# Last attention of a fused block stack: outputs with tokens on partitions, scaled per pair of heads and then transposed; gains folded into k and the rope tables

## The chip, the cores and the metric

The kernel runs on one core of one Trainium2 chip. The metric is the device time of one execution in microseconds, which is that of its only core. Five engines run side by side, each through its own list of instructions in order: TensorE (PE in the profile, its weight loads PEld), VectorE (DVE), ScalarE (ACT), GpSimd (POOL) and SyncE (SP), which issues the transfers from device memory.

## The reference

A stream of 256 tokens of width 1024 goes through two stacks of blocks. The change touches only the last attention, a sliding-window one with 16 query heads and 2 key/value heads of width 64, rope on the first 16 of the 64 columns, and one learned sink per head:

```
q = rms_norm_2(q, q_gain); k = rms_norm_2(k, k_gain)
q = apply_partial_rope(q, cos, sin); k = apply_partial_rope(k, cos, sin)
...
scores = jnp.einsum('bntkgd,bnskd->bnkgts', qb, k_band).astype(jnp.float32) * (HEAD_DIM ** -0.5)
mask = (k_pos >= 0) & (k_pos <= q_pos) & (q_pos - k_pos < WINDOW)      # WINDOW = BLOCK = 128
scores = jnp.where(mask[None, :, None, None], scores, -jnp.inf)
m = jnp.maximum(jnp.max(scores, axis=-1, keepdims=True), sink)
p = jnp.exp(scores - m)
probs = p / (jnp.sum(p, axis=-1, keepdims=True) + jnp.exp(sink - m))
o = jnp.einsum('bnkgts,bnskd->bntkgd', probs.astype(v_band.dtype), v_band)
return o.reshape(b, s, SW_Q_HEADS * HEAD_DIM) @ w_out
```

With 256 tokens there are two blocks of 128 queries. The first sees 128 keys, the second 256.

## The kernel before

All matrix products with weights are done in three matmuls, of a high and a low part of both sides (`mm3`, the lines L398 to L400). A weight tile `raw` comes by DMA, ACT writes its high part `wh` (L224), DVE the low part `wl` (L225). A product of activations needs the same split of the activations: `hilo` lets ACT write `ah` (L494) and DVE `al` (L495).

The stage in question is `window`. `in_fill` computes q, k and v (four groups of four query heads, and one group for k and v). `normed` makes the normed and rotated q or k of a group: DVE multiplies by the inverse norm (L1099), then the gain (L1101) and rope (L1104 to L1107) follow, on DVE for k and on POOL for the four groups of q. `transposed` turns the result over on PE (L1115) and lets ACT copy it (L1118).

Then come 16 heads in a software pipeline. Each head has four steps:

- s1: for an even head PE computes the scores `s` of it and of the next head (L1208, L1210), two heads at once since each uses 64 rows of the array. For every head DVE adds the mask and takes the row minimum of the negated scores (L622), ACT takes the exponentials `p` with their sums (L625), and the sink's term `es` (L1216).
- s1b: DVE adds the sink's term, takes the reciprocal and scales `p` by it (L1223 to L1226).
- s2: PE transposes `p` in three blocks (L1233), ACT copies them to `pt` (L1235).
- s3, for odd heads only: four matmuls with v as the stationary side and `pt` moving (L1245, L1247) give the outputs `o` of the pair, with the 64 columns of each head on partitions and the tokens along the rows; the two heads go to the two halves of the partitions. `hilo` splits them into `ah` and `al`, the pair's entry in `mix`.

No scheduler moves anything: the engines run in the order in which the code calls them. `pipeline` sets it. In round t it calls, by `SW_ORDER = "013..2"` and the lags (1, 2, 4): s1 of head t, s1b of head t-1, s3 of head t-4, then twice the filler, then s2 of head t-2. The filler is a generator of other matmuls, at first the rest of q, then `rows_steps`, the product of `mix` with the output weights: for pair c it takes two steps (tokens 0 to 127, then 128 to 255; six matmuls each) as soon as `mix[c]` is set in the program, which is when the instructions that make it have been written down, not when they have run. PE's matmuls wait for `ah` and `al` by semaphore. For the last four pairs the steps go another way: first the first half of the tokens of pairs 4 to 7, and at the end the second half.

Tiles in the eight PSUM banks come from two rings of four: `gbank` (ring "g") gives `s`, `pT`, `tp`, `o`; a new tile of a ring waits until the tile four requests earlier has been read.

## Time and profile before

| | us |
|---|---|
| three runs | 1604.93, 1600.98, 1604.84 (median 1604.84) |
| profiled execution, its own time | 1600.43 |
| its span (what the trace covers) | 1598.7 |
| PE busy in the span | 1582.0 (99%) |
| DVE, ACT, POOL busy | 967.4 (61%), 819.7 (51%), 46.9 (3%) |
| chain of work that ended last, by engine | PE 92%, DVE 5%, ACT 2% |

The stage `window` lies between about 1320 and 1405 us of the span. PE's busy time counts matmuls from start to a modelled end, so the work of a group is read better from the start of one group to the start of the next. In a row of the timeline, what stands in square brackets is how long the engine was idle before it and who released it; "x4" merges four records. One fp32 matmul of the program is two records on PE in these rows where its inputs are full fp32 (scores, outputs), and one for the split products.

### The profile page before, as it was taken

What the parts mean: (1) busy time and instruction counts of PE and PEld (TensorE: products, weight loads), DVE (VectorE), ACT (ScalarE), POOL (GpSimd) and SP (SyncE); (2) the same over time, 40 slices, a digit from 0 to 9 for tenths busy, and PEclk for the clock granted to TensorE, in tenths of its full rate; (3) what the DMA queues carried; (4) which work ended last, traced back from release to release, by engine and by line L of the source; (5) the groups of instructions that cost most, each with busy time, mean ns of one, the idle gap of its engine ahead of it and who ended that gap; (6) DMA issues with size and microseconds to landing.
All of it is one profiled execution on the core that took longest, in us unless ns stands there. A gap on an engine that the chain in (4) does not pass through costs nothing.

```text
span 1598.7 us, 27739 instructions
## 1 busy us (share of the span) xinstructions
PE 1582.0 (99%) x11230; PEld 1453.6 (91%) x11230; DVE 967.4 (61%) x1637; ACT 819.7 (51%) x1405; POOL 46.9 (3%) x70
## 2 busy tenths in 40 slices
PE   9999999999999999999999999999999999999999
PEld 8989999998799998999999889999999998699998
DVE  7786655578665556754564465555654558865553
ACT  6665444457554444544457765444444446754442
POOL 0101000000000000000000000000000002000000
PEclk9999999999999999999999999999999999999999
DMA  8545555553456554656545437556465554246552
GB/s 301 175 137 179 200 199 184 177 185 96 125 177 210 188 181 159 210 200 197 186 146 183 133 109 247 184 183 203 161 199 192 196 173 134 88 149 211 183 178 75
DMA packets 78946, 279.47 MB, mean 175 GB/s; under 512 B 9057, under 2 KB 10593, under 8 KB 78818
## 3 DMA queue, kind: packets, MB, share of 16 engines
q1 hardware_dynamic: 78050, 276.12, 52.6%
q0 software_dynamic: 768, 1.57, 0.5%
q8 instruction: 88, 1.44, 0.4%
q14 instruction: 40, 0.33, 0.1%
HBM read 276.61 MB, written 1.05 MB: 174 GB/s over the span
## 4 chain that ended last, share of the span: by engine, by line
PE 92%; DVE 5%; ACT 2%; issue 1%; DMA 1%; POOL 0%; SPq 0%; DVEq 0%; ACTq 0%; POOLq 0%
PE gu L398 16%; PE gu L400 16%; PE gu L399 16%; PE o L398 9%; PE o L399 9%; PE o L400 9%; DVE wl L225 2%; PE s L810 2%; PE k L398 1%; PE k L399 1%; PE k L400 1%; PE q L398 1%; PE q L399 1%; PE q L400 1%; PE v L398 1%; PE tp L368 1%
## 5 line engine op out<-in xcount | busy, mean ns | idle before, releaser
L225 DVE TENSOR_TENSOR wl<-raw,wh 128x1024 fp32r<-128x1024 f32 (+2 forms) x510 | 600.0, 1219 | 115.4 <-ACT wh L224 114.9
L398 PE MATMUL gu<-hh,wh 128*128 128x256 f32 x1920 | 540.4, 281 | 0.0
L400 PE MATMUL gu<-hl,wh 128*128 128x256 f32 x1920 | 539.6, 281 | 0.0
L399 PE MATMUL gu<-hh,wl 128*128 128x256 f32 x1920 | 539.1, 281 | 0.0
L224 ACT ACTIVATE wh<-raw 128x1024 fp32r<-128x1024 f32 (+2 forms) x510 | 506.5, 1043 | 44.8 <-DMA raw<-in_w_dram 26.6
L399 PEld LDWEIGHTS gu<-hh,wl 128*128 128x128 f32 x1920 | 361.9, 189 | 4.0
L398 PEld LDWEIGHTS gu<-hh,wh 128*128 128x128 f32 x1920 | 361.6, 188 | 4.0
L400 PEld LDWEIGHTS gu<-hl,wh 128*128 128x128 f32 x1920 | 361.8, 188 | 0.0
L552 ACT ACTIVATE sg<-gu 128x256 f32<-128x256 f32 x120 | 45.9, 383 | 426.3 <-PE gu L400 415.2
L398 PE MATMUL o<-wh,ah 128*128 128x512 f32 x656 | 260.0, 396 | 0.4 <-ACT ah L494 0.4
L399 PE MATMUL o<-wh,al 128*128 128x512 f32 x656 | 257.8, 393 | 0.0
L400 PE MATMUL o<-wl,ah 128*128 128x512 f32 x656 | 257.7, 393 | 0.0
L553 DVE TENSOR_TENSOR sg<-gu,sg 128x256 f32<-128x256 f32 x120 | 50.9, 424 | 295.9 <-ACT sg L552 295.8
L400 PEld LDWEIGHTS o<-wl,ah 128*128 128x128 f32 x656 | 123.1, 188 | 27.0
L398 PEld LDWEIGHTS o<-wh,ah 128*128 128x128 f32 x656 | 123.7, 189 | 25.6 <-issue 2.8
L399 PEld LDWEIGHTS o<-wh,al 128*128 128x128 f32 x656 | 123.2, 188 | 22.6 <-DVE al L495 0.5
L494 ACT ACTIVATE ah<-sg 128x256 fp32r<-128x256 f32 x120 | 50.1, 418 | 71.0 <-DVE sg L553 71.0
L495 DVE TENSOR_TENSOR al<-sg,ah 128x256 fp32r<-128x256 f32 x120 | 51.0, 425 | 58.1 <-ACT ah L494 58.1
L625 ACT ACTIVATE p<-p,mn 128x256 f32<-128x256 f32 x96 | 46.1, 481 | 30.3 <-DVE mn L622 30.1
L494 ACT ACTIVATE hh<-tp 128x512 fp32r<-128x512 f32 x40 | 23.2, 597 | 61.5 <-PE tp L368 61.3
L398 PE MATMUL gu<-wh,hh 128*128 128x256 f32 x192 | 54.7, 285 | 0.0
L399 PE MATMUL gu<-wh,hl 128*128 128x256 f32 x192 | 54.0, 282 | 0.0
(249 smaller groups left out, 1888.4 us busy)
## 6 DMA issues: line engine op xcount, KB each, us to landing
raw<-in_w_dram SPq DMA_DIRECT2D x498, 512.0 KB, 4.5
gb<-in_gains_dram SPq DMA_DIRECT2D x10, 512.0 KB, 5.0
raw<-in_w_dram SPq DMA_DIRECT2D x8, 416.0 KB, 5.3
hank<-in_t_dram SPq DMA_DIRECT2D x8, 192.0 KB, 4.2
hank<-in_rpb_dram POOLq DMA_DIRECT2D x16, 96.0 KB, 4.4
out_dram<-x SPq DMA_DIRECT2D x4, 256.0 KB, 2.0
raw<-in_w_dram SPq DMA_DIRECT2D x2, 384.0 KB, 4.7
x<-in_x_dram SPq DMA_DIRECT2D x2, 256.0 KB, 3.0
```

The costliest lines, as they stand in the source:

```text
L224: ACT.activation(out=hi, in_=src, func=AF.Copy)
L225: late.append(lambda: engine.tensor_tensor(out=lo, in0=src, in1=hi.bitcast(F32), op=ALU.subtract))
L368: PE.transpose(ps[:, k * 128:(k + 1) * 128], xn[:, k * 128:(k + 1) * 128], ident)
L398: PE.matmul(ps, lhsT=lh, rhs=rh, start=first, stop=False)
L399: PE.matmul(ps, lhsT=ll, rhs=rh, start=False, stop=False)
L400: PE.matmul(ps, lhsT=lh, rhs=rl, start=False, stop=last)
L494: ACT.activation(out=hi, in_=src, func=AF.Copy)
L495: DVE.tensor_tensor(out=lo, in0=src, in1=hi.bitcast(F32), op=ALU.subtract)
L552: ACT.activation(out=sg, in_=ps[:, 0:256], func=AF.Silu)
L553: DVE.tensor_tensor(out=sg, in0=ps[:, 256:512], in1=sg, op=ALU.mult)
L625: ACT.activation(out=p[:, sl], in_=p[:, sl], func=AF.Exp, scale=-1.0, bias=mn[:, b:b + 1], accum_out=sm[:, b:b + 1])
L810: PE.matmul(ps[:, i * 256:(i + 1) * 256], lhsT=q[pr, i * 128:(i + 1) * 128], rhs=k[pr, :], start=True, stop=True)
```

## The change

Three things change in `window` (and in `prepare_rope`, which fills tables much earlier, in the first feed-forward stage).

Outputs: `pt` becomes the stationary side and v the moving one. Per pair there are six matmuls of 64 columns in place of four (of 256 and 128 columns), and their output `o` has the tokens on partitions. DVE scales it into a tile `y` by the reciprocal sums of both heads. In the next even head's s3, a new function `turn` transposes `y` in two blocks on PE, and `hilo` reads those blocks instead of `o`. The pipeline gets a 17th, empty task so that the last pair's `turn` is called.

Sums: `p` is not scaled any more. The sink's term, its exponential, the sum and the reciprocal are computed once for a pair of heads (four columns) instead of once per head.

Rope and gains: on the 48 columns without rope the q gain is multiplied into the k gain; on the 16 with rope both gains go into two rope tables. The multiplication of q by its gain falls away, and q's rope runs on DVE instead of POOL.

```
+        for which, c in ((1, R_KG), (0, R_QG)):
+            DVE.tensor_tensor(out=rope[:, which], in0=rope[:, 0], in1=row[:, c:c + 16].unsqueeze(1).unsqueeze(1).to_broadcast([128, 2, 2, 16]),
+                              op=ALU.mult)
+        DVE.tensor_tensor(out=row[:, R_KG + 16:R_KG + 64], in0=row[:, R_KG + 16:R_KG + 64], in1=row[:, R_QG + 16:R_QG + 64], op=ALU.mult)
...
-        def normed(ps, heads, gcol, guess, engine=POOL):
+        def normed(ps, heads, which, guess):
...
-            engine.tensor_tensor(out=y3, in0=y3, in1=row[:, gcol:gcol + 64].unsqueeze(1).to_broadcast([128, n, 64]), op=ALU.mult)
+            if which:
+                DVE.tensor_tensor(out=y3[:, :, 16:64], in0=y3[:, :, 16:64],
+                                  in1=row[:, R_KG + 16:R_KG + 64].unsqueeze(1).to_broadcast([128, n, 48]), op=ALU.mult)
             t = wk.tile([128, 2, n, 16], F32, name="rts", tag="rtq", bufs=1)
             for j in range(2):
-                engine.tensor_tensor(out=t[:, j].rearrange("p (i h) d -> p i h d", i=2), in0=y[:, :, :, 0:16],
-                                     in1=rope[:, :, j].unsqueeze(2).to_broadcast([128, 2, heads, 16]), op=ALU.mult)
-            engine.tensor_tensor(out=y3[:, :, 0:8], in0=t[:, 0, :, 0:8], in1=t[:, 1, :, 8:16], op=ALU.subtract)
-            engine.tensor_tensor(out=y3[:, :, 8:16], in0=t[:, 0, :, 8:16], in1=t[:, 1, :, 0:8], op=ALU.add)
+                DVE.tensor_tensor(out=t[:, j].rearrange("p (i h) d -> p i h d", i=2), in0=y[:, :, :, 0:16],
+                                  in1=rope[:, which, :, j].unsqueeze(2).to_broadcast([128, 2, heads, 16]), op=ALU.mult)
+            DVE.tensor_tensor(out=y3[:, :, 0:8], in0=t[:, 0, :, 0:8], in1=t[:, 1, :, 8:16], op=ALU.subtract)
+            DVE.tensor_tensor(out=y3[:, :, 8:16], in0=t[:, 0, :, 8:16], in1=t[:, 1, :, 0:8], op=ALU.add)
...
-                mn, sm, rc, es = small(2, "mn"), small(2, "sm"), small(2, "rc"), small(2, "es")
-                softmax_rows(ps, WID, mn, p, sm, [cst[:, C_SW:C_SW + 256], cst[:, C_SW + 256:C_SW + 384]],
+                z = n % 2
+                if z == 0:
+                    state["sums"] = [small(4, name).rearrange("p (b z) -> p b z", z=2) for name in ("mn4", "sm4", "es4")]
+                mn, sm, es = state["sums"]
+                softmax_rows(ps, WID, mn[:, :, z], p, sm[:, :, z], [cst[:, C_SW:C_SW + 256], cst[:, C_SW + 256:C_SW + 384]],
                              start=nsink[:, n:n + 1])
-                ACT.activation(out=es, in_=mn, func=AF.Exp, bias=row[:, R_SI + n:R_SI + n + 1])
-                state[n] = p, sm, es, rc
+                state[n] = p
+                if z == 1:
+                    DVE.tensor_tensor(out=es, in0=mn, in1=row[:, R_SI + n - 1:R_SI + n + 1].unsqueeze(1).to_broadcast([128, 2, 2]),
+                                      op=ALU.add)
+                    ACT.activation(out=es, in_=es, func=AF.Exp)
+                    state["sums", n] = sm, es
...
             def s1b():
-                p, sm, es, rc = state[n]
-                DVE.tensor_tensor(out=sm, in0=sm, in1=es, op=ALU.add)
-                DVE.reciprocal(out=rc, in_=sm)
-                for b in range(2):
-                    DVE.tensor_scalar(out=p[:, WID[b]], in0=p[:, WID[b]], scalar1=rc[:, b:b + 1], scalar2=None, op0=ALU.mult)
-                state[n] = p
+                if n % 2:
+                    sm, es = state["sums", n]
+                    DVE.tensor_tensor(out=sm, in0=sm, in1=es, op=ALU.add)
+                    DVE.reciprocal(out=sm, in_=sm)
...
             def s3():
                 if h % 2 == 0:
+                    turn()
                     return
                 ps = gbank("o")
...
                 for z in range(2):
-                    PE.matmul(ps[PAIR[z], 0:256], lhsT=v[0], rhs=pts[z][:, 0:256], start=True, stop=False)
-                for z in range(2):
-                    PE.matmul(ps[PAIR[z], 128:256], lhsT=v[1], rhs=pts[z][:, 256:384], start=False, stop=True)
-                a = act_tiles()
-                hilo(ps[:, 0:256], *a)
-                mix[n // 2] = a
+                    o = ps[:, z * 64:z * 64 + 64]
+                    PE.matmul(o, lhsT=pts[z][:, 128:256], rhs=v[0], start=True, stop=False)
+                    PE.matmul(o, lhsT=pts[z][:, 256:384], rhs=v[1], start=False, stop=True)
+                    PE.matmul(ps[:, 128 + z * 64:192 + z * 64], lhsT=pts[z][:, 0:128], rhs=v[0], start=True, stop=True)
+                y = wk.tile([128, 2, 2, 64], F32, name="y", tag="v", bufs=3)
+                sm, _ = state.pop(("sums", n))
+                DVE.tensor_tensor(out=y, in0=ps[:, 0:256].rearrange("p (b z d) -> p b z d", b=2, z=2),
+                                  in1=sm.unsqueeze(3).to_broadcast([128, 2, 2, 64]), op=ALU.mult)
+                state["y"] = n // 2, y
...
+        def turn():
+
+            if "y" not in state:
+                return
+            k, y = state.pop("y")
+            ps = gbank("oT")
+            for b in range(2):
+                PE.transpose(ps[:, (1 - b) * 128:(2 - b) * 128], y[:, b].rearrange("p z d -> p (z d)"), ident)
+            a = act_tiles()
+            hilo(ps[:, 0:256], *a)
+            mix[k] = a
...
-        pipeline([head(n) for n in range(16)], fill, SW_RATE, SW_LAG, SW_ORDER)
+        pipeline([head(n) for n in range(16)] + [(nothing, nothing, nothing, turn)], fill, SW_RATE, SW_LAG, SW_ORDER)
```

Where this puts the instructions, at three places. First PE in round t = 10, where the scores of heads 10 and 11 are computed and the filler begins on the pair c = 2. The numbers after the names tell one tile from another. Before, from the outputs of that pair on:

```order
L1245 MATMUL o_15316<-pt_15220,v_14725 64x256
L1245 MATMUL o_15316<-pt_15260,v_14725 64x256
L1247 MATMUL o_15316<-pt_15220,v_14725 64x128
L1247 MATMUL o_15316<-pt_15260,v_14725 64x128
...
L1233 MATMUL pT_15336<-cst_64,p_15222 128x128 x3
L1208 MATMUL s_15342<-qk_14863,qk_15126 128x256
L1208 MATMUL s_15343<-qk_14863,qk_15126 128x256
L1210 MATMUL s_15342<-qk_14863,qk_15126 128x128
L1210 MATMUL s_15343<-qk_14863,qk_15126 128x128
L398 MATMUL o_15206<-wh_14905,ah_15321 128x512
L399 MATMUL o_15206<-wh_14905,al_15322 128x512
```

There ACT and DVE make `ah_15321` and `al_15322` straight from `o_15316`. Now, on PE in the same round:

```order
L1240 MATMUL pT_15296<-cst_64,p_15193 128x128 x3
L1210 MATMUL s_15302<-qk_14865,qk_15104 128x256
L1210 MATMUL s_15303<-qk_14865,qk_15104 128x256
L1212 MATMUL s_15302<-qk_14865,qk_15104 128x128
L1212 MATMUL s_15303<-qk_14865,qk_15104 128x128
L1272 MATMUL oT_15319<-cst_64,y_15283 128x128 x2
L398 MATMUL o_15177<-wh_14906,ah_15322 128x512
L399 MATMUL o_15177<-wh_14906,al_15323 128x512
```

The pair's first filler matmuls stood three groups (`pT`, `s` and a filler step) behind the outputs from which their input is made; now they stand right behind the two transposes from which it is made. So it is for the pairs 0 to 3.

Second, ACT in that round (`p` with its sums are the exponentials of a head, `pt` the copy of transposed probabilities, `wh` a weight split). Before:

```order
L625 ACTIVATE p_15302,sm_15304<-p_15302,mn_15303 128x256
L625 ACTIVATE p_15302,sm_15304<-p_15302,mn_15303 128x128
L1216 ACTIVATE es_15306<-mn_15303,row_65 128x2
L494 ACTIVATE ah_15321<-o_15316 128x256
L224 ACTIVATE wh_15333<-raw_14976 128x1024
L1235 ACTIVATE pt_15340<-pT_15336 128x384
L625 ACTIVATE p_15348,sm_15350<-p_15348,mn_15349 128x256
L625 ACTIVATE p_15348,sm_15350<-p_15348,mn_15349 128x128
```

Now, from the weight split of round 9 to the copy of round 10:

```order
L224 ACTIVATE wh_15293<-raw_14976 128x1024
L1242 ACTIVATE pt_15300<-pT_15296 128x384
L625 ACTIVATE p_15308,sm4_15310<-p_15308,mn4_15309 128x256
L625 ACTIVATE p_15308,sm4_15310<-p_15308,mn4_15309 128x128
L494 ACTIVATE ah_15322<-oT_15319 128x256
L1242 ACTIVATE pt_15336<-pT_15332 128x384
```

The split `ah` stood behind the exponentials of an odd head (9), whose scores had been computed a round earlier; now it stands behind those of the even head (10), whose scores are computed in this round.

Third, DVE in round 6, where the norm and rope of the last group of q fall. Before, between the split of pair 0 and the row minima of head 6:

```order
L495 TENSOR_TENSOR al<-o,ah 128x256
L290 TENSOR_TENSOR rt<-ry 128x8
L291 TENSOR_TENSOR rt<-rt,rh 128x8
L292 SCALAR_TENSOR_TENSOR rz<-rt,ry 128x8
L1099 TENSOR_TENSOR qn<-qkv,rz 128x256 x2
L622 ISA p,mn<-s,cst,nsink 128x256
```

Now, at the same place:

```order
L1259 TENSOR_TENSOR y<-o,sm_14990 128x256
L290 TENSOR_TENSOR rt<-ry 128x8
L291 TENSOR_TENSOR rt<-rt,rh 128x8
L292 SCALAR_TENSOR_TENSOR rz<-rt,ry 128x8
L1099 TENSOR_TENSOR qn<-qkv,rz 128x256 x2
L1106 TENSOR_TENSOR rts<-qn,rope 128x128 x2
L1108 TENSOR_TENSOR qn<-rts 128x8x8
L1109 TENSOR_TENSOR qn<-rts 128x8x8
L622 ISA p,mn_15161<-s,cst,nsink 128x256
```

The rope's four instructions have come in ahead of head 6's row minima, and the pair's `al` has gone behind them.

## Rows read from the trace of the kernel before

**Rows 1.** Windows of 2.5 us of the stage: us from the span's start, length, then busy time and instructions of PE, PEld, DVE, ACT and POOL, the granted TensorE clock, DMA share and GB/s.

```profile
1347.50:1350.00 2.50, 0.35 (x4) 0.22 (x4) 1.82 (x6) 1.17 (x4) 2.34 (x5) 1.00 0.59 152
...
1360.00:1362.50 2.50, 2.50 (x14) 1.42 (x12) 2.40 (x11) 2.09 (x8) 0.00 (x0) 0.53 0.65 177
...
1375.00:1377.50 2.50, 2.50 (x18) 1.85 (x17) 1.07 (x4) 2.35 (x8) 0.00 (x0) 1.00 0.67 210
```

**Rows 2.** Waits of PE between 1340 and 1400 us: engine, tile and line that waited, what it waited for, us in total, times, longest.

```profile
PE s L1208 <- ACT qk L1118: 2.1, 1, 2.1
PE pT L1233 <- DVE p L1226: 1.7, 2, 1.1
PE tp L1115 <- DVE al L495: 0.8, 1, 0.8
PE o L1245 <- ACT pt L1235: 0.7, 2, 0.4
PE s L1208 <- DVE mn L622: 0.6, 1, 0.6
PE s L1208 <- ACT pt L1235: 0.4, 1, 0.4
PE o L398 <- ACT ah L494: 0.4, 1, 0.4
```

**Rows 3.** Timeline of PE in the steady part, one pair: start, us, engine, line, operation, tiles, shape, count.

```profile
1376.21 0.49 PE L1233 MATMUL pT<-cst,p 128*128 128x128 f32 x3
1376.63 0.70 PE L1208 MATMUL s<-qk 64*128 64x256 f32 x4
...
1377.48 0.50 PE L398 MATMUL o<-wh,ah 128*128 128x512 f32 x1
...
1378.98 0.49 PE L1233 MATMUL pT<-cst,p 128*128 128x128 f32 x3
1379.40 0.65 PE L1245 MATMUL o<-pt,v 128*64 128x256 f32 x4
...
1380.20 0.50 PE L398 MATMUL o<-wh,ah 128*128 128x512 f32 x1
```

**Rows 4.** Timeline of PE in the first attention stage, where two kinds of work stand that the change adds here: four matmuls of 64 columns with a transposed probability tile as the stationary side (L917), and four transposes of a finished output (L942), each with the row that follows it.

```profile
81.05 1.10 PE L917 MATMUL o<-v,pt 128*128 128x64 f32 x8
81.97 0.36 PE L398 MATMUL v<-wh,hh 128*128 128x256 f32 x1
...
85.31 1.00 PE L917 MATMUL o<-v,pt 128*128 128x64 f32 x8
86.14 0.61 PE L836 MATMUL pT<-cst,p 128*128 128x128 f32 x4
...
104.93 0.66 PE L942 MATMUL oT<-cst,on 128*128 128x128 f32 x4
105.34 0.48 PE L398 MATMUL o<-wh,ah 128*128 128x512 f32 x1
```

**Rows 5.** Timeline of PE, DVE and ACT around the scores of heads 12 and 13: the scores, the row minima of head 12, the scaling of head 11, a weight split, and ACT's exponentials of head 12 up to its sink term.

```profile
1382.11 0.70 PE L1208 MATMUL s<-qk 64*128 64x256 f32 x4
...
1383.07 0.48 DVE L622 CUSTOM_DVE_ANT_0 p<-s,cst,nsink 128x256 f32<-128x256 f32 x1 [0.39 <-PE s L1210]
...
1383.75 0.16 DVE L1223 TENSOR_TENSOR sm<-sm,es 128x2 f32<-128x2 f32 x1
...
1384.61 1.22 DVE L225 TENSOR_TENSOR wl<-raw,wh 128x1024 fp32r<-128x1024 f32 x1
1385.74 0.48 DVE L622 CUSTOM_DVE_ANT_0 p<-s,cst,nsink 128x256 f32<-128x256 f32 x1
...
1383.60 0.51 ACT L625 ACTIVATE p<-p,mn 128x256 f32<-128x256 f32 x1
...
1384.49 0.28 ACT L1216 ACTIVATE es<-mn,row 128x2 f32<-128x2 f32 x1
```

**Rows 6.** Timeline of ACT, DVE and PE at the first split of an output in this stage: `ah`, `al`, and the matmul that waited for `ah`.

```profile
1364.48 0.37 ACT L494 ACTIVATE ah<-o 128x256 fp32r<-128x256 f32 x1
...
1364.88 0.42 DVE L495 TENSOR_TENSOR al<-o,ah 128x256 fp32r<-128x256 f32 x1 [0.69 <-ACT ah L494]
...
1364.90 0.49 PE L398 MATMUL o<-wh,ah 128*128 128x512 f32 x1 [0.40 <-ACT ah L494]
```

**Rows 7.** Timeline of DVE and ACT: k's rope (the first row; it ends where the copy of k begins), the norm of q's last group up to the next head's row minima, and the step of ACT ahead of the copy of q that the first scores wait for.

```profile
1338.26 0.36 DVE L1104 TENSOR_TENSOR rts<-qn,rope 128x64 f32<-128x64 f32 x2
...
1338.99 0.43 DVE L1125 COPY k<-qn 128x512 f32<-128x512 f32 x1
...
1365.22 0.16 DVE L290 TENSOR_TENSOR rt<-ry 128x8 f32<-128x8 f32 x1
...
1366.55 0.48 DVE L622 CUSTOM_DVE_ANT_0 p<-s,cst,nsink 128x256 f32<-128x256 f32 x1
...
1348.80 0.21 ACT L1088 ACTIVATE ry<-rh 128x8 f32<-128x8 f32 x1 [2.14 <-DVE rh L1085]
```

**Rows 8.** Timeline of PE at the end of the heads: the outputs of the last two pairs, each with the row that follows it.

```profile
1391.76 0.65 PE L1245 MATMUL o<-pt,v 128*64 128x256 f32 x2
...
1393.64 0.50 PE L398 MATMUL o<-wh,ah 128*128 128x512 f32 x1
...
1395.56 0.65 PE L1245 MATMUL o<-pt,v 128*64 128x256 f32 x2
...
1397.26 0.50 PE L398 MATMUL o<-wh,ah 128*128 128x512 f32 x1
```

More of the change, by code (lines that the diff above doesn't have):

```diff
@@ L264 @@
     lam = pc.tile([128, 2], F32, name="lam")
-    rope = pc.tile([128, 2, 2, 16], F32, name="rope")
+    rope = pc.tile([128, 2, 2, 2, 16], F32, name="rope")
     def small(w, name):
@@ L1122, in kv_done @@
             ps3 = ps.rearrange("p (i c) -> p i c", i=2)
-            y = normed(ps3[:, :, 0:128].rearrange("p i (h d) -> p i h d", h=2), 2, R_KG, guess, DVE)
+            y = normed(ps3[:, :, 0:128].rearrange("p i (h d) -> p i h d", h=2), 2, 1, guess)
             k4 = wk.tile([128, 2, 4, 64], F32, name="k4", tag="p", bufs=5)
@@ L1143, in done @@
                 def done(guess):
-                    qn[g] = normed(ps4, 4, R_QG, guess, POOL)
+                    qn[g] = normed(ps4, 4, 0, guess)
                 return squares(ps4, 4, done)
@@ L1244, in s3, with nothing @@
                 for z in range(2):
-                    PE.matmul(ps[PAIR[z], 0:256], lhsT=v[0], rhs=pts[z][:, 0:256], start=True, stop=False)
-                for z in range(2):
-                    PE.matmul(ps[PAIR[z], 128:256], lhsT=v[1], rhs=pts[z][:, 256:384], start=False, stop=True)
-                a = act_tiles()
-                hilo(ps[:, 0:256], *a)
-                mix[n // 2] = a
-            return s1, s1b, s2, s3
-        pipeline([head(n) for n in range(16)], fill, SW_RATE, SW_LAG, SW_ORDER)
+                    o = ps[:, z * 64:z * 64 + 64]
[7 more added lines that the diff above has]
+                state["y"] = n // 2, y
+            return s1, s1b, s2, s3
+        def turn():
[8 more added lines that the diff above has]
+            mix[k] = a
+        def nothing():
+            pass
+        pipeline([head(n) for n in range(16)] + [(nothing, nothing, nothing, turn)], fill, SW_RATE, SW_LAG, SW_ORDER)
         fill.until("out")
@@ L1365, in prepare_rope @@
             for half in range(2):
-                ACT.activation(out=rope[:, :, j, 8 * half:8 * half + 8], in_=a, func=AF.Sin)
+                ACT.activation(out=rope[:, 0, :, j, 8 * half:8 * half + 8], in_=a, func=AF.Sin)
+        for which, c in ((1, R_KG), (0, R_QG)):
+            DVE.tensor_tensor(out=rope[:, which], in0=rope[:, 0], in1=row[:, c:c + 16].unsqueeze(1).unsqueeze(1).to_broadcast([128, 2, 2, 16]),
+                              op=ALU.mult)
+        DVE.tensor_tensor(out=row[:, R_KG + 16:R_KG + 64], in0=row[:, R_KG + 16:R_KG + 64], in1=row[:, R_QG + 16:R_QG + 64], op=ALU.mult)
     chores = [lambda h=h: prepare_diff(h) for h in range(4)]
```

## The prediction

> **What bounds the kernel now.** PE does, nearly everywhere, and the change can only be worth what PE does or waits for in the stage `window`. I read three views in this order. The windows of the stage [rows 1] show where PE is not full: 0.35 of 2.5 us at 1347.5, and a stretch at 1360 in which the granted clock is 0.53, so partly at the lower of its two levels. In the steady part (1375) PE is full and DVE busy 1.07 of 2.50. The table of PE's waits [rows 2] gives the sizes: 6.7 us in nine waits. The 2.1, 1.1, 0.6 and 0.4 (on `qk`, `p`, `mn` and the early `pt`) lie before 1363.6, where the fourth pair's scores start; 0.4 (`ah`), 0.8 (`al`), 0.6 (the second wait on `p`) and 0.7 (`pt`) after it. The timeline [rows 3] shows a steady pair with no gap: transposes 0.42 (1376.21 to 1376.63), scores 0.85, a filler step 1.50 (1377.48 to 1378.98), transposes 0.42, outputs 0.80 (1379.40 to 1380.20). There a microsecond taken from DVE or ACT gives nothing, and one added to PE costs one.
>
> **PE's own work.** The outputs of a pair are now six matmuls of 64 columns with a 128-column stationary side. The trace has four of that kind in a row: 0.92 us (81.05 to 81.97) and 0.83 (85.31 to 86.14) [rows 4], so six are 1.24 to 1.38; I take 1.30, which is 0.50 more than 0.80. Four transposes of a finished output take 0.41 (104.93 to 105.34), so two take 0.2. From the fourth pair's scores on there are seven outputs and eight double transposes: 3.5 + 1.6 = **+5.1** (bounds 4.7 and 5.7). The first outputs fall before it, where ACT and DVE set the pace.
>
> What the Trainium skill would make of this: "TensorEngine Tiling (Array Packing)", When to Use Tiling, wants a product whose moving side has 64 columns swapped and put on two column tiles, which is the form of before; if undoing that doubled the 0.80, the seven would cost 5.6 instead of 3.5 and the time below would be 2.1 us higher. The rows of L917 are nearer than that.
>
> **The new wait.** This term decides. In rounds 6, 8, 10 and 12 the filler's first matmul on pair c now stands directly behind the transposes that feed it (PE's order above), and needs `ah`, which ACT makes only after the exponentials of the even head (ACT's order). Those need that head's row minima, and those the scores that PE did just ahead. Before, `ah` came from outputs a round earlier, with a filler step, transposes and scores in between.
>
> The chain is priced from the scores' start at 1382.11 [rows 5]: DVE's minima start at 1383.07 (+0.96), the exponentials at 1383.60, and ACT is free for the next step at 1384.49, +2.38. From the start of `ah` to the matmul that waits for it: 1364.48 to 1364.90, 0.42 [rows 6]. So the filler can begin 2.80 after the scores' start. PE has scores (0.85) and two transposes (0.2) to do, 1.05: it idles **1.75**. Behind it L399 needs `al`. In rounds 8, 10 and 12 a weight split `wl` (1.13, 1384.61 to 1385.74) is now ahead of `al` on DVE: minima until +1.63, pair sum and reciprocal about 0.36 (the nearest rows: two of the four scaling instructions between 1383.75 and 1384.61), `wl` until +3.1, `al` 0.42 until +3.55. L399 would else begin about 0.34 after L398, at +3.14, so 0.45 more.
>
> - Round 6: DVE still has `y`, the norm of q's last group and its rope ahead of head 6's minima. The norm takes 1.33 (1365.22 to 1366.55), the rope about 0.9 (k's takes 0.73, 1338.26 to 1338.99 [rows 7], and q's has 192 more columns at about 1 ns, since `wl` takes 1.13 for 1,024). With `y` at 0.35 (estimated from `al`, whose 0.42 has the same size) DVE is 2.6 late from the end of the outputs, some 0.25 before the scores start: minima at +2.35 instead of +0.96. Wait 1.75 + 1.4 = 3.1.
> - Round 8: the transposes of q's last group (0.4) are on PE's side, the copy of them (about 0.5) on ACT's: 1.75 - 0.4 + 0.5 = 1.85, and `al` is then no later.
> - Rounds 10 and 12: 1.75 + 0.45 = 2.2 each.
>
> Together **+9.3** (bounds 7.0, four waits of 1.75, and 10.5, if `al` comes late in rounds 6 and 8 too).
>
> **The end of the heads.** With no filler between rounds 13 and 16, four waits follow. The transposes of head 13 use the bank of head 15's scores, whose minima stand on DVE behind a `wl` and an `al`: about 1.25. The next transposes wait for `y`: 0.2. Later `y` of pair 6 is queued behind two `wl` (2 x 1.13), 1.0; the last pair has outputs, `y` and transposes in a row, 0.6. Together **+3.0** (bounds 1.5 and 3.5).
>
> **Waits that go.** Scaling `p` and most of the small sums leave DVE: 0.86 for each head (1383.75 to 1384.61), against 0.5 a pair that come back and one `y`. So the waits on `p`, `al`, `pt` and `ah` after 1363.6 go as they were, 2.5, and with them the slow outputs at the end: 1.88 (1391.76 to 1393.64) and 1.70 (1395.56 to 1397.26) [rows 8] against 0.80 each are 1.98 of excess, of which 0.7 is counted. Together **-3.8** (bounds -3.0 and -4.6).
>
> **The start.** POOL's rope isn't what the first scores wait for. They wait for a copy of q that ACT does behind L1088, which waits 2.14 for DVE's sums of the group after next [rows 7]; two ropes of 0.9 now lie ahead of these on DVE. So the first wait grows by up to 1.8, less what DVE gains where POOL no longer runs beside it. Afterwards DVE saves five scalings (4.3) and pays a third rope, the pair sums and `y`, and the pair's sum waits for `es` of two heads. It comes out about even: **+0.2** at the fourth pair's scores. Bounds: -2.0, half of the 4.2 of early waits, and +1.8. The new code in `prepare_rope` is three small DVE instructions in a stage that PE fills: nothing. POOL's queue loses its rope and gains nothing.
>
> **The sum.** 0.2 + 5.1 + 9.3 + 3.0 - 3.8 = +13.8 us. On the profiled execution this is 1600.43 + 13.8 = 1614.2, on the median 1604.84 + 13.8 = 1618.6. The four executions lie at two levels 4 us apart (1600.4 and 1601.0, 1604.8 and 1604.9) and I can't tell on which the next falls: between them, **1616**. About 0.3% (4.8 us) is what a measurement of this kernel can tell from no change.
>
> **The rivals.**
>
> - *Not slower: the waits of before go and none comes.* If ACT had `ah` ready within the 1.05 us that PE works from the scores on, the filler would not stall, and the end would be as smooth. Then -2.0 (half the early waits) + 5.1 - 3.8 leaves -0.7: 1600 to 1604. For it: DVE loses 8.8 us of scaling, and its share is highest where PE waits. Against: `ah` takes 2.80 in the rows, and ACT takes its steps in order. It decides in favour of this only below 1.05. Chance 0.07.
> - *Half the wait.* Minima and exponentials could run closer together with DVE emptier, and `wl` could be done before `al` is due: stalls of 0.9 instead of 1.75 to 3.1, and 1.5 at the end. 0.2 + 5.1 + 3.6 + 1.5 - 3.8 = +6.6: 1607 to 1611. Against: DVE was idle 0.39 when the scores came [rows 5], so that chain was already at its shortest. Chance 0.13.
> - *The clock falls in the new stalls.* At 1360 the clock stood at 0.53 after waits of 1.1 and 0.6 close together; after the 2.1 at 1347.5 it held 1.00 [rows 1, 2]. The stall of 3.1 in round 6, followed by smaller ones, is longer than either. Two and a half microseconds at about half the clock lose some 1.2; two or four such stretches make +2.5 to +5: 1618 to 1623. Chance 0.15.
> - *PE works past a waiting matmul*, so that the stalls are filled by the transposes and outputs behind. Then 9.3 of the sum goes: +4.5, 1605 to 1609. Against: at 1347.5 PE stood for 2.1 with filler matmuls for q behind the waiting scores [rows 1, 2]. The Trainium skill, "TensorE: Matmul & The Clock Gate", specification table, speaks of a partial reorder window that pulls weight loads ahead of matmuls in flight; by that rule, taken at its widest, this is the case. Chance 0.03.
>
> **How the numbers follow.** The forecast has 0.62. Its bounds, all low or all high at once, add to +6.6 and +18.5. The range must hold 8 in 10: it reaches from 1608 (+7 on the low level, where the low sum and the second rival's lower half lie) to 1623 (the high sum on the high level, and the forecast with a fallen clock), and leaves out the first rival, part of the second and the last. Slower by over 0.3%: 0.62 + 0.15 + 0.11 of the second and 0.01 of the last, 0.89. Within: 0.06 of the first, 0.02 and 0.02 of those two, 0.10. Faster: 0.01.
>
> **What would show it.** In PE's waits, filler L398 on `ah` with four waits of 1.7 to 3.1, and L399 on `al` behind some; outputs of 1.2 to 1.4 us from their start to the next group; the waits on `p` gone; the first scores' wait on `qk` at 2.1 or longer. The steady pair should grow from 5.5 to over 8 us. It is wrong if L398 shows no wait on `ah`, if outputs take under 1 us, or if the stage's end doesn't move while its waits do.

## The result, and the profile after

| | us |
|---|---|
| kernel before, four runs on the same chip | 1604.93, 1600.98, 1604.84, 1600.13 (median 1602.91) |
| changed kernel, four runs | 1618.10, 1623.13, 1620.84, 1619.03 (median 1619.93) |
| ratio | 1.0107, 95% interval 1.0090 to 1.0124 |
| profiled execution of the changed kernel, its span | 1618.10, 1616.3 |

The change makes the kernel about 17 us slower, by more than the 0.3% that can be told from no change. The forecast was 1616 with a range of 1608 to 1623.

Where the time went can be read from three marks on PE, present in every kernel of this study: the transposes of q's first group (mark T), the scores of the fourth pair (mark 4), and the first `gu` product of the next stage (mark G). T itself lies between 1346 and 1352 us in the traces of this study, also where the work ahead of it is the same, so only distances between marks are compared. The three marks of the kernel before, then of the changed one:

```profile
1347.04 0.60 PE L1115 MATMUL tp<-cst,qn 128*128 128x128 f32 x4
...
1363.57 0.70 PE L1208 MATMUL s<-qk 64*128 64x256 f32 x4 [0.42 <-ACT pt L1235]
...
1407.89 0.28 PE L398 MATMUL gu<-wh,hh 128*128 128x256 f32 x1
```

```profile
1349.03 0.60 PE L1117 MATMUL tp<-cst,qn 128*128 128x128 f32 x4
...
1365.76 0.70 PE L1210 MATMUL s<-qk 64*128 64x256 f32 x4
...
1425.56 0.28 PE L398 MATMUL gu<-wh,hh 128*128 128x256 f32 x1
```

| kernel | T | 4 | G | T to 4 | 4 to G | T to G |
|---|---|---|---|---|---|---|
| before | 1347.04 | 1363.57 | 1407.89 | 16.53 | 44.32 | 60.85 |
| changed | 1349.03 | 1365.76 | 1425.56 | 16.73 | 59.80 | 76.53 |

So 15.7 us are lost between T and G, and all but 0.2 of them after the fourth pair's scores.

PE's waits between 1340 and 1420 us in the changed kernel (engine, tile and line that waited, what it waited for, us in total, times, longest), the same view as [rows 2]:

```profile
PE o L398 <- ACT ah L494: 7.4, 4, 2.8
PE s L1210 <- ACT qk L1120: 2.8, 1, 2.8
PE oT L1272 <- DVE y L1259: 2.4, 3, 1.0
...
PE o L399 <- DVE al L495: 0.5, 2, 0.2
```

In [rows 2] the filler L398 waited 0.4 in all, once; now it is 7.4 in four waits. No wait on `p` is in the list any more. The timeline shows how one comes about, in round 10 (PE first, then DVE, then ACT), with round 6 ahead of it; it answers to [rows 3] and [rows 5]:

```profile
1366.61 0.44 PE L1272 MATMUL oT<-cst,y 128*128 128x128 f32 x2
1369.89 0.80 PE L398 MATMUL o<-wh,ah 128*128 128x512 f32 x1 [2.84 <-ACT ah L494]
...
1372.65 0.56 PE L1240 MATMUL pT<-cst,p 128*128 128x128 f32 x3
...
1384.65 0.70 PE L1210 MATMUL s<-qk 64*128 64x256 f32 x4
...
1385.51 0.44 PE L1272 MATMUL oT<-cst,y 128*128 128x128 f32 x2
1387.44 0.49 PE L398 MATMUL o<-wh,ah 128*128 128x512 f32 x1 [1.50 <-ACT ah L494]
1388.17 0.50 PE L399 MATMUL o<-wh,al 128*128 128x512 f32 x1 [0.24 <-DVE al L495]
...
1389.78 0.33 PE L1254 MATMUL o<-v,pt 128*128 128x64 f32 x2
...
1391.04 0.48 PE L398 MATMUL o<-wh,ah 128*128 128x512 f32 x1
...
1392.94 0.70 PE L1210 MATMUL s<-qk 64*128 64x256 f32 x4
...
1368.06 0.48 DVE L622 CUSTOM_DVE_ANT_0 p<-s,cst,nsink 128x256 f32<-128x256 f32 x1
...
1385.61 0.48 DVE L622 CUSTOM_DVE_ANT_0 p<-s,cst,nsink 128x256 f32<-128x256 f32 x1 [2.17 <-PE s L1212]
...
1386.57 1.21 DVE L225 TENSOR_TENSOR wl<-raw,wh 128x1024 fp32r<-128x1024 f32 x1
...
1386.13 0.51 ACT L625 ACTIVATE p<-p,mn 128x256 f32<-128x256 f32 x1 [0.82 <-DVE mn L622]
...
1387.03 0.36 ACT L494 ACTIVATE ah<-oT 128x256 fp32r<-128x256 f32 x1
```

Read down the chain: scores 1384.65, minima 1385.61, exponentials 1386.13, `ah` 1387.03, filler 1387.44. DVE and ACT are idle before their parts (2.17 and 0.82), so nothing else holds them up: it is the length of the chain. The six output matmuls take 1.26 (1389.78 to 1391.04), where [rows 3] has 0.80. A steady pair takes 8.29 us (1384.65 to 1392.94) instead of 5.5.

One thing stands in the windows (2.5 us each; columns as in [rows 1]) that the sum of the forecast left to a rival. The granted clock, the third number from the end, is 0.50 in three of them, the lower of its two levels (1.2 of 2.4 GHz). Each follows a wait: the first scores' 2.80, round 6's 2.84, and round 12's 1.50.

```profile
1352.50:1355.00 2.50, 2.50 (x13) 2.10 (x14) 1.98 (x7) 0.82 (x1) 0.00 (x0) 0.50 0.33 129
...
1370.00:1372.50 2.50, 2.50 (x6) 1.89 (x7) 1.13 (x6) 0.00 (x0) 0.00 (x0) 0.50 0.00 0
...
1397.50:1400.00 2.50, 2.50 (x12) 2.11 (x10) 0.00 (x0) 0.45 (x2) 0.00 (x0) 0.50 0.46 184
```

In the second of them a filler step that takes 1.50 in [rows 3] takes 2.76 (1369.89 to 1372.65 in the timeline above).

### The profile page after: what moved, and what is told of

Read it like the earlier page. It is cut to its first block, busy times and chain, and to the rows that moved or that the text cites. A ratio compares the mean times of both kernels' runs of the same rounds, so it can differ in the third digit from the quotient of the medians.

```text
span 1616.3 us, 27783 instructions
## 1 busy us (share of the span) xinstructions
PE 1590.5 (98%) x11278; PEld 1463.9 (91%) x11278; DVE 963.3 (60%) x1624; ACT 818.2 (51%) x1397; POOL 33.2 (2%) x50
## 3 DMA queue, kind: packets, MB, share of 16 engines
HBM read 276.61 MB, written 1.05 MB: 172 GB/s over the span
## 4 chain that ended last, share of the span: by engine, by line
PE 92%; DVE 4%; ACT 2%; DMA 1%; issue 1%; POOL 0%; SPq 0%; DVEq 0%; ACTq 0%; POOLq 0%
PE gu L398 15%; PE gu L400 15%; PE gu L399 15%; PE o L399 9%; PE o L398 9%; PE o L400 9%; DVE wl L225 2%; PE s L810 2%; PE k L398 1%; PE k L399 1%; PE k L400 1%; PE q L398 1%; PE q L399 1%; PE q L400 1%; DMA raw<-in_w_dram 1%; PE v L398 1%
## 5 line engine op out<-in xcount | busy, mean ns | idle before, releaser
L398 PE MATMUL gu<-hh,wh 128*128 128x256 f32 x1920 | 540.2, 281 | 0.0
L399 PE MATMUL gu<-hh,wl 128*128 128x256 f32 x1920 | 538.9, 281 | 0.0
L399 PEld LDWEIGHTS gu<-hh,wl 128*128 128x128 f32 x1920 | 361.8, 188 | 4.0
L398 PEld LDWEIGHTS gu<-hh,wh 128*128 128x128 f32 x1920 | 361.4, 188 | 4.0
L398 PE MATMUL o<-wh,ah 128*128 128x512 f32 x656 | 260.8, 397 | 7.4 <-ACT ah L494 7.4
L399 PE MATMUL o<-wh,al 128*128 128x512 f32 x656 | 259.0, 395 | 0.5 <-DVE al L495 0.5
L398 PEld LDWEIGHTS o<-wh,ah 128*128 128x128 f32 x656 | 124.0, 189 | 32.4 <-ACT ah L494 8.5
L399 PEld LDWEIGHTS o<-wh,al 128*128 128x128 f32 x656 | 123.6, 188 | 24.2 <-DVE al L495 2.1
L398 PE MATMUL gu<-wh,hh 128*128 128x256 f32 x192 | 54.7, 285 | 0.0
L399 PE MATMUL gu<-wh,hl 128*128 128x256 f32 x192 | 54.0, 281 | 0.0
```

What stands on the lines that cost most here:

```text
L398: PE.matmul(ps, lhsT=lh, rhs=rh, start=first, stop=False)
L399: PE.matmul(ps, lhsT=ll, rhs=rh, start=False, stop=False)
```

## The experiments

The theory: where dependent work was put in the three queues (`oT` behind the scores on PE, `ah` behind the even head's exponentials on ACT) makes the stalls, and they cost their own length plus the clock that falls after some. The rivals: PE's extra work is the cost and the waits only show it; VectorE's rope is a main cost; ACT is the bound.

### The turn ahead of the scores

```
-SW_ORDER = "013..2"
+SW_ORDER = "301..2"
```

> The changed kernel with one table entry changed: in each round of the head pipeline the step s3 (outputs or turn) is called ahead of s1 (scores, minima, exponentials). No instruction is added or removed; the transposes of a finished output stand ahead of the next scores on PE, and ah stands ahead of the even head's exponentials on ACT. My theory (the order of dependent work made the stall): the four waits of L398 on ah, 7.4 us in the changed kernel, all but go (under 1 us left), the clock does not fall at 1370 and 1397 any more (2 to 3 us), and the outputs still take 1.26 us; 8 to 11 us faster than the changed kernel, ratio to the kernel before 1.001 to 1.006. Rival (the extra work of PE, small matmuls and transposes, is the cost, and the waits only show where PE would have waited anyway): the waits move to another place, the scores or the transposes, and the time changes by less than 3 us, ratio 1.009 to 1.011.

Measured: ratio to the kernel before 1.0060 (1.0045 to 1.0075), some 7.5 us faster than the changed kernel, a little under the 8 to 11 that I gave; T to G 69.92. The theory's direction holds and the rival's does not, but the waits did not go as I said: 2.1 are left, one of them in this round (waits, then timeline of PE and ACT).

```profile
PE o L398 <- ACT ah L494: 2.1, 3, 0.8
```

```profile
1386.70 0.49 PE L398 MATMUL o<-wh,ah 128*128 128x512 f32 x1 [0.78 <-ACT ah L494]
...
1384.97 1.04 ACT L224 ACTIVATE wh<-raw 128x1024 fp32r<-128x1024 f32 x1
1385.91 0.47 ACT L1242 ACTIVATE pt<-pT 128x384 f32<-128x384 f32 x1
1386.29 0.36 ACT L494 ACTIVATE ah<-oT 128x256 fp32r<-128x256 f32 x1
```

`ah` is now queued behind a weight split and a copy. I had taken one thing out of its way on ACT and not looked at what else stood there.

### The split handed on a round later

```
+        def publish():
+            if "done" in state:
+                k, a = state.pop("done")
+                mix[k] = a
...
             def s3():
                 if h % 2 == 0:
                     turn()
                     return
+                publish()
...
-            mix[k] = a
+            state["done"] = k, a
+            if k == 7:
+                publish()
```

> The changed kernel, with a pair's ah and al handed to the filler one round later (in the next odd head's s3) and all orders of ACT and DVE kept. On PE a filler step, transposes and outputs now stand between the turned output and the first filler matmul on it. My theory: the waits of L398 on ah (7.4 us) go, since ah is still made as late as before but is no longer needed at once; but one pair less of filler work is ready at each moment, so the end of the heads may keep or gain up to 3 us of waits. 5 to 10 us faster than the changed kernel, ratio 1.001 to 1.006. Rival (PE's extra work): under 3 us, 1.009 to 1.011. A second rival, that ACT is the bound of the steady rounds (its order is unchanged here): PE then waits the same 1.5 us a pair at the transposes or the scores, and the time stays.

Measured: 1.0028 (1.0015 to 1.0040), about 12 us faster than the changed kernel, more than the 5 to 10 that I gave; T to G 64.76. PE's waits, and two rows of its timeline:

```profile
PE s L1210 <- ACT qk L1120: 3.0, 1, 3.0
PE o L1255 <- DVE mn L622: 1.4, 2, 1.3
...
```

```profile
1381.13 0.70 PE L1210 MATMUL s<-qk 64*128 64x256 f32 x4
...
1387.13 0.70 PE L1210 MATMUL s<-qk 64*128 64x256 f32 x4
```

No wait of L398 is left. The orders of ACT and DVE did not stay quite as I said: the weight splits go with the filler, and now stand behind the split of the pair (`ah` at 1383.51, `wh` at 1383.77; `al` at 1383.90, `wl` at 1385.12). But ACT has the same steps to do for a pair, so it was no bound. A steady pair is 6.00 us against 8.29: 0.5 more than the 5.5 of before. That 0.5 is what PE's own work adds. It settles the main question: of the 15.7 us between T and G, 11.8 hang on when the split is needed (with the weight splits that moved along), with every instruction of the change still there.

### Each part alone

The first kernel is the one before with only the rope part, the second the changed kernel without it. Their edits are the hunks of the diff above from `normed` and `prepare_rope`, put in and taken out:

```
-                    qn[g] = normed(ps4, 4, R_QG, guess, POOL)
+                    qn[g] = normed(ps4, 4, 0, guess)
```

> The kernel before with only the rope part of the change: gains folded into k and the rope tables, rope of q on VectorE; outputs, sums and scaling of p as before. My theory: about nothing, ratio 0.999 to 1.002; the first scores' wait on qk (2.1 before) grows by 0 to 1.8, and the filler and outputs look as before. Rival (rope on VectorE is a main cost, since VectorE is busy for the whole first part of the stage): +4 us or more, ratio 1.003 to 1.006, with the extra in the waits of scores and transposes before 1364.

> The changed kernel with the rope part taken back: q's gain and rope on GpSimd as in the kernel before; outputs, turn and sums per pair as in the changed kernel. My theory: nearly all of the cost is here, ratio 1.008 to 1.011; the first wait of L398 on ah (2.84 in the changed kernel) falls to about 1.5 to 1.8, since q's last rope no longer stands ahead of head 6's minima; the other three stay at 1.5. Rival (rope on VectorE is a main cost): ratio 1.005 or less.

Measured: rope alone 1.0012 (1.0000 to 1.0024), outputs alone 1.0090 (1.0075 to 1.0106). Most of the cost is in the outputs part, as expected: T to G takes 63.00 and 72.82, so 2.2 and 12.0 of the 15.7 us. Mark T and mark 4 of both, rope alone first:

```profile
1350.81 0.60 PE L1117 MATMUL tp<-cst,qn 128*128 128x128 f32 x4
...
1369.70 0.70 PE L1210 MATMUL s<-qk 64*128 64x256 f32 x4 [0.49 <-ACT pt L1237]
```

```profile
1351.16 0.60 PE L1115 MATMUL tp<-cst,qn 128*128 128x128 f32 x4
...
1366.17 0.70 PE L1208 MATMUL s<-qk 64*128 64x256 f32 x4
```

From T to 4 these are 18.89 and 15.01, against 16.53 before and 16.73 with both. So the start is no place where nothing happens: with rope on VectorE it is 2.4 longer, with the outputs part 1.5 shorter. How much of that is the clock's is not separated. The granted clock fell in other windows in each of the three (to 0.53 at 1360 before, to 0.50 from 1355 to 1360 with rope alone and from 1355 to 1357.5 with the outputs alone), and a kernel further down, with rope on GpSimd and the split later, has the same work up to mark 4 as the outputs alone but takes 16.79 for it, with the clock at 0.50 from 1362.5 to 1367.5. The first wait of L398 fell from 2.84 to 2.00 only, not to the 1.5 to 1.8 that I gave: the rope's 0.8 is gone (1367.26 to 1368.06 in the changed kernel), but the norm still stands ahead of the minima.

### The first wait, taken out of ACT's queue

The 2.15 on `qk` in the kernel before, and the 2.97 with the later split, come from a copy behind L1088. Both kernels got the same move:

```
-        steps(SW_PRE[2])
+        steps(SW_PRE[2] - 2)
+        for _ in range(2):
+            fill.step()
         q_ready(0)
```

> The kernel before with one move: the first group of q is transposed and copied before the norm chores of the group after next, whose L1088 on ACT waited 2.14 ahead of that copy. No work is added or removed. If the first scores' wait is only that queue: the wait on qk falls from 2.15 to about 0.6, and the time falls by 1.5 to 3 us, ratio 0.998 to 0.999. Rival: VectorE, which works without a gap there, hands the delay on; the wait comes back at the transposes of p or at the next scores and the time stays within 1 us.

> The kernel with the split handed on a round later (outputs, sums and rope as in the changed kernel), with the same move as the run above. There the first wait is 2.97 and the clock stands at 0.50 for two windows after it. If the clock's fall comes from that wait: the wait shrinks to about 0.7, no window stands at 0.50, and the time falls by 4 to 6 us, to a ratio of 0.999 to 1.001 of the kernel before. If the clock falls for another reason: only the wait's 2.3 us go, ratio 1.001 to 1.002. If VectorE hands the delay on: under 1 us.

Measured: 1.0011 (1.0001 to 1.0020) and 1.0044 (1.0032 to 1.0057). Both are slower, against both of my main expectations. The first timeline is of the kernel before with the move, the waits and windows behind it of the other:

```profile
1352.35 0.70 PE L1210 MATMUL s<-qk 64*128 64x256 f32 x4 [0.69 <-ACT qk L1118]
...
1355.25 1.11 PE L1115 MATMUL tp<-cst,qn 128*128 128x128 f32 x4 [1.98 <-POOL qn L1107]
```

```profile
PE pT L1242 <- ACT p L625: 2.4, 1, 2.4
PE s L1212 <- DVE mn L622: 1.8, 1, 1.8
```

```profile
1365.00:1367.50 2.50, 2.50 (x14) 2.18 (x11) 2.43 (x10) 2.50 (x10) 0.00 (x0) 0.50 0.74 193
...
1377.50:1380.00 2.50, 2.50 (x9) 1.73 (x9) 0.00 (x0) 0.38 (x1) 0.00 (x0) 0.50 0.00 0
```

The wait went as planned (0.69), and a wait of the same size came back at the next thing that the other engines had not done: POOL's rope of group 1 in the one, `p` and the minima in the other. There the clock then stood at 0.50 in six windows in a row (1365 to 1380, of which the first and the last are shown), with PE busy all the time. T to 4 did not get shorter but longer, 18.70 against 16.53 and 18.94 against 16.94. So the queue that PE happens to wait for does not set the pace of the first four pairs; the chain through the other engines does, though the clock's part in these distances is not separated. In the second kernel the clock has its own price behind that: the two pairs after mark 4 take 8.87 and 7.03, against 6.47 and 6.43 with the later split alone, 3.0 of the 5.0 us by which T to G is longer (69.74 against 64.76).

### The stalls filled

```
+                    if n == 0:
+                        busy(state["s"][0], 24)
...
-                ps = gbank("pT")
+                ps = state.pop("pT", None)
+                if ps is None:
+                    ps = gbank("pT")
...
+            if k < 4:
+                state["pT"] = gbank("pT")
+                busy(state["pT"], 24 if k == 0 else 12)
...
+        def busy(ps, n):
+            for _ in range(n):
+                PE.matmul(ps[:, 0:256], lhsT=maskb[:, 0], rhs=maskb.rearrange("p a b -> p (a b)"), start=True, stop=True)
```

> The changed kernel with matmuls that nobody reads (128x256, bf16, 0.11 us each) put where TensorE stands still: 24 ahead of the first scores, 24 ahead of the first filler matmul on pair 0, 12 ahead of those on pairs 1 to 3. They write into a bank that the next transposes or scores overwrite. No wait of another engine changes. If the clock's three falls are a cost of their own (one of my rivals in the prediction): the granted clock stays at 1.00 in the three stretches, and the time falls by 3 to 5 us although PE does more, ratio 1.007 to 1.009. If the falls cost nothing on the path, or the stalls are the only loss: no change or up to 1 us slower, 1.010 to 1.012.

Measured: 1.0092 (1.0078 to 1.0106), 2.4 us less than the changed kernel where I gave 3 to 5. The two intervals overlap, so the times alone don't decide; the trace does. No window of the stage is under 1.00. T to G is 74.06 against 76.53, and the 2.5 us are just where the clock had fallen: from the fourth to the fifth pair's scores 9.33 against 10.43, from the seventh to the eighth 8.26 against 9.86, and the two distances between them are the same within 0.02. The scores of the fifth pair in the changed kernel, then those of the fourth and fifth here, with a window between them:

```profile
1376.19 0.70 PE L1210 MATMUL s<-qk 64*128 64x256 f32 x4
```

```profile
1368.86 0.70 PE L1212 MATMUL s<-qk 64*128 64x256 f32 x4
...
1378.19 0.70 PE L1212 MATMUL s<-qk 64*128 64x256 f32 x4
```

```profile
1370.00:1372.50 2.50, 2.48 (x24) 2.08 (x22) 2.10 (x11) 0.94 (x5) 0.00 (x0) 1.00 0.00 0
```

The filler on pair 0 starts 3.28 after the transposes ahead of it in both (1369.71 to 1372.99 here), so the wait itself is as long as it was. The first stretch gave nothing (T to 4 is 16.94): with the clock kept up, PE came to this wait instead.

```profile
1364.93 0.48 PE L1212 MATMUL s<-qk 64*128 64x256 f32 x1 [1.54 <-ACT pt L1246]
```

So the two later falls cost 1.1 and 1.6, and the one in the start cost nothing: the other engines set the pace there.

### The mild forms together, and what is left

The later split with q's gain and rope on GpSimd; then the same with 18 filling matmuls ahead of the first scores; then with a second filling, at the scores of heads 4 and 5 (the filling matmuls are 128x128 in this one, 28 of them ahead of the first scores):

```
                         PE.matmul(ps[:, 0:256], lhsT=q[pr, 128:256], rhs=k[pr, :], start=True, stop=True)
+                        if n == 4 and ps is state["s"][0]:
+                            busy(ps, 18)
```

> The two milder parts put together: the split handed on a round later, and q's gain and rope on GpSimd as in the kernel before. If the costs add as in the stage's rows (the later split left +2.8 in a thousand of the kernel before, the rope part accounts for 1 to 1.7 of those), the ratio is 1.001 to 1.002: TensorE's own extra work of some 5 us is left, less the waits that the change removes. If the rope part's cost was only the first wait, which other work hides, the ratio stays at 1.0025 or more.

> The same kernel with 18 matmuls that nobody reads (128x256, bf16) ahead of the first scores, where TensorE waits 2.2. If the clock's fall after that wait is on the path, it goes and the time falls by 1 to 2 us against the run beside it. If VectorE and ScalarE set the pace of the first four pairs, the clock stays at 1.00, TensorE waits longer for them a little later, and the time is the same within 0.7 us.

> The run before this one (later split, rope on GpSimd, first wait filled) with a second filling: 18 matmuls of 128x128 that nobody reads, between the two first score matmuls of heads 4 and 5, where TensorE waited 1.3 to 1.5 and the clock fell afterwards, from 1360 to 1367, over windows in which TensorE was busy all the time. If that fall is on the path: the clock stays at 1.00 and 2 to 3 us go, ratio 0.9990 to 1.0000, a version no slower than the kernel before. If the first pairs are paced by VectorE and ScalarE there too: another wait takes its place, ratio 1.001 to 1.002 as before.

Measured: 1.0013 (1.0000 to 1.0026), 1.0013 (1.0003 to 1.0022), and 0.9999 (0.9991 to 1.0008). The first comes out as expected. The second shows the wait moved again (2.1 on `qk` became 0.2, and 1.3 on `mn` became this, with the clock at 0.50 behind it):

```profile
PE s L1210 <- ACT pt L1242: 1.5, 1, 1.5
```

```profile
1362.50:1365.00 2.50, 2.50 (x13) 1.77 (x12) 1.87 (x7) 0.49 (x1) 0.61 (x1) 0.50 0.01 3
```

The third filled that wait too, and every window of the stage is at 1.00:

```profile
1362.50:1365.00 2.50, 2.18 (x20) 1.94 (x19) 2.40 (x13) 2.47 (x10) 0.00 (x0) 1.00 0.71 223
```

T to G falls from 63.87 and 64.10 to 61.85: 2 us, so this fall of the clock was on the path; what is left is 1.0 more than before. Most of it lies ahead of mark 4, where T to 4 goes from 16.79 and 16.52 to 15.03. With the outputs alone, where the clock had fallen earlier and was back, it was 15.01, so an early fall seems to be hidden there, a late one not. This version has the new outputs and sums, with rope and q's gain as before, and is as fast as the kernel before; it does not beat it.

The same filling in the kernel before, 12 matmuls at a wait of 1.05 and 8 at one of 0.57:

> The kernel before with the same kind of filling: 12 matmuls of 128x128 that nobody reads ahead of the transposes of head 1 (a wait of 1.05) and 8 between the first score matmuls of heads 4 and 5 (0.57), after which its clock fell to 0.53 (1.7 us of lost work in two windows). If that loss is on the path: 1 to 2 us faster, ratio 0.9988 to 0.9995. If VectorE and ScalarE pace that part: no change, 0.9995 to 1.0005.

Measured: 1.0003 (0.9995 to 1.0012). It decides little, since the clock fell elsewhere: after the first scores' wait, which I had not filled because in the profile of before it stood at 1.00 there.

```profile
1351.07 0.70 PE L1208 MATMUL s<-qk 64*128 64x256 f32 x4 [2.15 <-ACT qk L1118]
```

```profile
1352.50:1355.00 2.50, 2.50 (x13) 2.35 (x12) 2.21 (x10) 1.24 (x6) 2.42 (x3) 0.50 0.33 64
```

## Why the prediction was right, term by term

The new waits are measured here as the forecast counted them, from the start of the group ahead plus its own time (0.2 for two transposes).

| term | forecast | measured | from |
|---|---|---|---|
| start, to the fourth pair's scores | +0.2 | +0.2 | 16.73 against 16.53 |
| PE's own work | +5.1 | about +4.2 | 0.52 a pair (6.00 against the 5.48 of before), eight pairs |
| the new wait | +9.3 | +9.1 | rounds 6 to 12: 3.08, 1.72, 2.12, 2.13 |
| end of the heads | +3.0 | +3.0 | 0.23, 1.14, 0.92, 0.71 |
| waits that go | -3.8 | about -4.1 | what remains in the kernel with the later split (below) |
| the clock after the stalls | a rival | +2.7 | 1.1 and 1.6, the stalls filled |
| sum | +13.8 | +15.1 | 15.7 between T and G |

**The new wait** was the deciding term, and its rows came as written. From the scores' start to the filler's the forecast had 2.80; it is 2.79 (1384.65 to 1387.44). `ah` begins 2.38 after them, as computed. `wl` stands ahead of `al`, so L399 starts 0.73 after L398 (0.34 elsewhere). In round 6 `y`, the norm and the rope put the minima 2.30 after the scores (1365.76 to 1368.06), forecast 2.35.

**PE's own work.** The six outputs take 1.26 (forecast 1.30). By the 2x that the Trainium skill, "TensorEngine Tiling (Array Packing)", When to Use Tiling, gives for the swapped form of before, undoing the swap would take twice 0.80; the runs here show a factor of 1.6. What I over-counted is the rest: next to the new outputs the three transposes take 0.33 instead of 0.42 (1381.19 to 1381.52, against 1378.98 to 1379.40 in [rows 3]), and the filler steps lose a few hundredths, so that a pair gains 0.52 and not 0.66.

**The start** came out even, as forecast. That it is +0.2 to the digit is luck: the bounds were -2.0 and +1.8, the parts alone show +2.4 and -1.5, and the same work took 15.01 in one kernel and 16.79 in another. That rope and scaling balance, the reason given, is not shown.

**Waits that go.** Between 4 and G the later split takes 47.82, 3.5 more than before. Its own work is 4.2, and its waits, counted as above, are 1.4 (transposes at 1369.62, outputs only at 1371.45) and 2.0 (the end); so about 4.1 have gone.

**The end** has the right sum and wrong places. The wait of 1.25 for the bank of head 15's scores did not come: the transposes of head 13 follow the outputs without a gap at 1405.97, before DVE begins the minima of head 15 (1406.19), so they did not wait for that bank. What stood ahead on DVE was waited for one step later, at `y`, with 1.02 instead of 0.2.

```profile
1405.74 0.39 PE L1256 MATMUL o<-v,pt 128*128 128x64 f32 x2
1405.97 0.55 PE L1240 MATMUL pT<-cst,p 128*128 128x128 f32 x3
1407.53 0.44 PE L1272 MATMUL oT<-cst,y 128*128 128x128 f32 x2 [1.02 <-DVE y L1259]
```

**The step that was off** is the clock. It was set apart as a rival with 0.15, as if it excluded the forecast; it came on top of it, with three stretches of which two cost 2.7 us, inside the 2.5 to 5 given there, and the measured 1619.93 lies in that rival's 1618 to 1623, above the forecast's 1616. The sum held the term at nothing, though the forecast itself produced a stall longer than those after which the clock had been seen to fall. That the total still came within 2 us of the 15.7 is helped by the 0.9 that PE's own work had too much. One bound was added wrongly: `al` late in rounds 6 and 8 too makes the new wait 10.2, not 10.5; nothing hangs on it.

**The other rivals.** *No new wait* and *half the wait* fall with four waits of the forecast size. *PE works past a waiting matmul* falls too: at 1387.44 PE had idled 1.5 us, with transposes of `p` further down its list that needed nothing of `ah`. The partial reorder window of the Trainium skill, "TensorE: Matmul & The Clock Gate", specification table, which is said there to pull weight loads ahead of running matmuls, is not seen to fill this stall.

What stays open: 0.6 of the 15.7 us is in no term, the waits that go are known only as a remainder, the two sides of the start are not parted from the clock, and the ratio's 17 us (14.4 to 19.9) is no sharper than the 15.7 of the two traces.

## What to carry to other kernels

When a step is put between a product and its use, write down for each engine what stands ahead of the new step in that engine's order, and count from the latest thing it depends on; handing the result on one round later gave back 11.8 of 15.7 us here. A wait that comes from a step queued behind another is worth removing only if the other engines do not set the pace behind it: twice here a wait of about the same size came back at the next group. With a stall on TensorE, count also what the clock may do after it, and look whether TensorE has to wait for other engines there anyway: a fall in such a place cost nothing, the others 1.1 to 1.6 us each.

## What the hardware showed beyond that

The length of a wait did not decide whether the clock fell. The first scores waited 2.1 to 2.2 in four kernels: the clock stood at 1.00 afterwards in the kernel before and with the later split and rope on GpSimd, and at 0.50 with the outputs alone and in the kernel before with its later waits filled. A wait of 1.50 was followed by a fall in round 12 of the changed kernel, the same 1.50 in round 10 by none, and one of 2.00 in round 6 of the outputs alone by none. Once fallen, it was back at 0.98 in the window after 1397.5 to 1400 in the changed kernel, but stayed at 0.50 for six windows in the later split with the moved copy of q, although PE was busy for 2.50 of 2.50 us in each. Matmuls that nobody reads (bf16, 0.11 us for 128x256 and 0.06 for 128x128) held it at 1.00 wherever they filled a wait.
